# Down product of the small expert tiles: two 128-wide products in place of three, with an addition where the result leaves PSUM

## The chip, the cores and the metric

The kernel runs on one core of a Trainium2 chip as one launch. The metric is device time in microseconds (us) from the start to the end of that launch. A core has a matrix engine (PE, with its weight loads shown apart as PEld), a vector engine (DVE), a scalar engine (ACT), a general engine (POOL), and SP, which here only issues transfers. Each engine works through its own instruction stream in order, and they meet at semaphores. Matrix products end in PSUM, which has eight banks of 128 partitions by 512 fp32 values; everything else lives in SBUF.

## The reference

The program is two blocks after one another, on 256 tokens of width 1024 (and, in the second block, 256 context tokens). The first block is two layers of a swiglu network, retention and forgetting attention. The second is two layers of attention with a routed network behind each. The change touches only the routed network:

```
def moe_ffn(h, w_router, router_bias, w_gate, w_up, w_down):
    s = sigmoid(h @ w_router)                    # 16 experts in 4 groups; the best group, then 2 of its 4
    ...
    for e in range(N_EXPERTS):
        y = (silu(h @ w_gate[e]) * (h @ w_up[e])) @ w_down[e]      # 1024 -> 512 -> 1024
        out = out + gates[:, e:e + 1] * y
```

Layer 0 routes 512 tokens (latent and context), layer 1 routes 256. All inputs and weights are fp32.

## The kernel before

**Two-part numbers.** Every weight tile arrives as fp32 (`raw`, 128x1024, 512 KB), and is split into a rounded part `whi` (ACT, line 188) and the rest `wlo` (DVE, line 190: `wlo = raw - whi`). Activations are split the same way (`split`, lines 366 and 367). A product is then three matmuls into one bank (`mm3`, lines 334 to 336): high by high, high by low weight, low by high weight. In a matmul the activation is the stationary operand (up to 128 columns, one per token slot), and the weights stream past it as the moving operand, 512 columns at a time.

**Routed layers.** Each expert has a fixed number of slots by its rank in load: rank 0 is the fullest. Layer 0 has ten tiles of 80 to 128 slots and six of 64 (ranks 9 to 14). Layer 1 has two experts of two 128-slot tiles each (ranks 0 and 1), two of one 128-slot tile (2 and 3), four of 64 slots (4 to 7) and eight of 32 (8 to 15). Tiles of at most 64 slots are called small here; their entry in `TILES` has `None` as its fourth member. There are 6 in layer 0 and 12 in layer 1. For gate and up the small tiles already put the high and the low part of the token slots side by side as one stationary operand (line 1725, two matmuls of 2n columns); the two halves are summed later by a small matmul against a folding matrix (`folded`, line 1738).

**A step.** `moe` goes through the experts in the order of `ORDER`: layer 0 by ranks 15, 9, 0, 10, 11, 1, 12, 2, 3, 4, 5, 14, 7, 6, 13, 8; layer 1 by 4, 5, 0, 6, 7, 8, 1, 9, 10, 11, 2, 12, 3, 13, 14, 15. The step of an expert is: its gate product (four weight tiles), its up product (four), then the down product `Dn` of the expert before it (four), then the folding or transposing of its own hidden values (`trans`) and their split into `hth` and `htl` (`stored`). Where an expert has two tiles, `Dn` of the one before comes between gate and up. Where the next expert begins a new group of slots, four gathers (line 1707, a product with a one-hot matrix) are placed in the step: two before `Dn` and two behind it.

**Order of work.** `between` converts at most one more weight tile ahead (`pump`) each time PE is given a weight tile, so in each engine's stream the conversions stand between everything else: twelve `whi` on ACT and twelve `wlo` on DVE for every expert. At most five converted tiles are ahead of PE (`ahead`).

**The down product.** `Dn` (lines 1749 to 1778) takes two PSUM banks of the tag `acc` for each tile, which has four banks in all and is shared with the gathers. For each of four weight tiles and two halves of 512 columns it does one `mm3`: 24 matmuls. ACT then copies both halves to an SBUF tile `y` (line 1772; line 1777 in a layer's last expert), and the store of `y` to a scratch tensor `Y` is issued from ACT's own queue (line 1773). At the end of the layer, `combine` gathers each token's two rows of `Y` and adds them.

Of the kernel before, what the change touches and what calls it, by code (L numbers as in the profile page):

```python
# [25 lines left out]
FR = mybir.dt.float32r  # L26
# [3 lines left out]
OP = mybir.AluOpType  # L30
# [58 lines left out]
PLACE, TILES, RUNS = zip(*map(layout, PAIRS))  # L89
# [154 lines left out]
class Kernel:  # L244
# [1437 lines left out]
    def moe(self, l, h2):  # L1682
        nc, W, I, T = self.nc, self.W, self.I, self.T
        V, S, PE = nc.vector, nc.scalar, nc.tensor
# [47 lines left out]
        hT, T1, T2 = {}, {}, {}  # L1732

        def folded(x, n):

            q = self.bank("tr", [128, 4, n], name="fold")
            for i in range(4):
                PE.matmul(q[:, i, :], x[:2 * n, i * 128:(i + 1) * 128], self.fold[n][:2 * n], start=True, stop=True)
            return q
# [8 lines left out]
            return y  # L1748

        def stored(e, i, p, n):  # L1750
            hT[e, i] = (self.k2([128, 4, n], FR, name="hth"), self.k2([128, 4, n], FR, name="htl"))
            self.split(hT[e, i][0], hT[e, i][1], p)

        def Dn(e):
            p, ts = place[e][0], TILES[l][e]
            w = W.next(4)
            b = [[self.bank("acc", [128, 512]) for _ in range(2)] for _ in ts]
            for k in range(4):
                self.between()
                for i, t in enumerate(ts):  # L1760
                    x = hT[e, i]
                    for n in range(2):
                        c = slice(n * 512, n * 512 + 512)
                        self.mm3(b[i][n][:t[1]], (x[0][:, k, :], x[1][:, k, :]), (w[k][0][:, 0, c], w[k][1][:, 0, c]),
                                 k == 0, k == 3)
                W.rel()
            for i, (c, n, _, _) in enumerate(ts):
                rows = Y[p * 256 + c:p * 256 + c + n, :]
                if e != seq[-1]:
                    y = self.k4([128, D], name="y")  # L1770
                    for x in range(2):
                        S.copy(y[:n, x * 512:(x + 1) * 512], b[i][x][:n])
                    S.dma_start(rows, y[:n])
                else:
                    for x in range(2):
                        y = self.k2([128, 512], name="y")
                        S.copy(y[:n], b[i][x][:n])
                        S.dma_start(rows[:, x * 512:(x + 1) * 512], y[:n])
                del hT[e, i]

# [7 lines left out]
        for j, e in enumerate(seq):  # L1788
            p, ts = place[e][0], TILES[l][e]
# [14 lines left out]
            if len(ts) > 1 and last is not None:  # L1804
                self.drain()
                Dn(last)
                last = None
# [5 lines left out]
            for i, (t, q) in enumerate(zip(ts, ps)):  # L1813
                if t[3] is None:
                    hs.append(copied(q, t[1]))
                    q = folded(us[i], t[1])
# [6 lines left out]
            def trans(i, e=e, ts=ts, us=us, hs=hs):  # L1823
                n = ts[i][1]
                if ts[i][3] is None:
                    q = folded(hs[i], n)
                    V.scalar_tensor_tensor(us[i], q, 0.5, us[i], op0=OP.mult, op1=OP.mult)
                    stored(e, i, us[i], n)
                else:
                    stored(e, i, self.transp([hs[i][:n, k * 128:(k + 1) * 128] for k in range(4)]), n)  # L1830
# [4 lines left out]
            if last is not None:  # L1835
                Dn(last)
# [9 lines left out]
        W.depth(*DEPTHS["end"])  # L1846
        self.drain()
        Dn(last)
        XT.clear()
        if MORE[l] and not self.dbg.get("noov"):  # L1850
# [420 lines left out]
```

## Time and profile before

| what | us |
| --- | --- |
| three runs | 2446.01, 2446.01, 2438.97 (median 2446.01) |
| profiled execution, its own time | 2443.65 |
| its span, from first to last instruction | 2441.9 |
| PE busy, weight loads busy | 2235.7, 1792.4 |
| DVE busy | 1831.4 |
| ACT busy | 1288.0 |

The profile shows one execution. Busy time is a sum over instructions; idle time in front of an instruction is put down to the engine whose semaphore came last. Matmuls are pipelined: one of 512 columns is shown as some 390 ns long although the next may start some 230 ns after it, so the pace of PE is read from starts, not from durations. Routed layer 0 takes the stretch from about 1505 to 1810 us, routed layer 1 that from about 2095 to 2407 us.

### The profile page before, as it was taken

The numbers are of one execution on the slowest core, as the hardware profiler recorded it, in microseconds if no ns is written. First come the engines' busy times: TensorE is split into PE (matmuls) and PEld (weight loads), VectorE is DVE, ScalarE is ACT, GpSimd is POOL, SyncE is SP. The second block draws the span as 40 slices with busy tenths as digits, with TensorE's granted clock in tenths as the row PEclk, the third lists the DMA queues.
The fourth block names the chain that finished last, engine by engine and source line by source line (L and its number), as shares of the span: only waits on it lengthen the run. The fifth ranks groups of instructions, "written<-read, shape, count | busy, mean of one in ns | idle before, by whom it ended". The sixth has DMA issues, their size and how long they took to land. (4 is left out here: it accounts for less than half of the span.)

```text
span 2441.9 us, 32688 instructions
## 1 busy us (share of the span) xinstructions
PE 2235.7 (92%) x11071; PEld 1792.4 (73%) x11071; DVE 1831.4 (75%) x2734; ACT 1288.0 (53%) x1931; POOL 226.0 (9%) x533
## 2 busy tenths in 40 slices
PE   6999999999999999999998988999958977799993
PEld 5888787788788888888776767678737856677662
DVE  5787778887877766886668767888866476877796
ACT  4445454444444545444347525787855343677783
POOL 2003002000200301210100011000020011100000
PEclk9999999999999999999999998999979988899997
DMA  9786557779787657787611125999982320888994
GB/s 278 240 236 202 150 172 237 226 235 286 263 262 229 197 151 217 215 241 236 196 52 35 52 78 178 346 346 316 352 313 70 124 67 1 318 322 288 338 391 162
DMA packets 247555, 526.06 MB, mean 215 GB/s; under 512 B 22817, under 2 KB 42193, under 8 KB 247377
## 3 DMA queue, kind: packets, MB, share of 16 engines
q1 hardware_dynamic: 232160, 479.87, 61.2%
q0 software_dynamic: 9616, 29.46, 3.5%
q10 hardware_dynamic: 5601, 14.54, 1.6%
q8 instruction: 91, 1.49, 0.2%
q14 instruction: 87, 0.71, 0.1%
HBM read 503.23 MB, written 20.53 MB: 214 GB/s over the span
## 5 line engine op out<-in xcount | busy, mean ns | idle before, releaser
L190 DVE TENSOR_TENSOR wlo<-raw,whi 128x1024 fp32r<-128x1024 f32 (+1 forms) x828 | 975.5, 1209 | 184.5 <-ACT whi L188 177.0
L188 ACT CAST whi<-raw 128x1024 fp32r<-128x1024 f32 (+1 forms) x828 | 827.9, 1043 | 165.6 <-PE mm L335 39.7
L334 PE MATMUL mm<-whi,xth 128*128 128x512 f32 (+3 forms) x1152 | 445.7, 387 | 10.7 <-ACT whi L188 6.1
L336 PE MATMUL mm<-whi,xtl 128*128 128x512 f32 (+3 forms) x1152 | 431.7, 375 | 0.1
L335 PE MATMUL mm<-wlo,xth 128*128 128x512 f32 (+3 forms) x1152 | 430.6, 374 | 0.5 <-DVE wlo L190 0.5
L334 PEld LDWEIGHTS mm<-whi,xth 128*128 128x128 f32 x1152 | 218.1, 189 | 48.4 <-ACT whi L188 6.5
L334 PE MATMUL acc<-whi,hth 128*128 128x512 f32 (+4 forms) x624 | 248.0, 397 | 5.3 <-ACT whi L188 2.7
L335 PE MATMUL acc<-wlo,hth 128*128 128x512 f32 (+4 forms) x624 | 245.3, 393 | 0.5 <-DVE wlo L190 0.5
L336 PE MATMUL acc<-whi,htl 128*128 128x512 f32 (+4 forms) x624 | 245.4, 393 | 0.0
L336 PEld LDWEIGHTS mm<-whi,xtl 128*128 128x128 f32 x1152 | 217.8, 189 | 37.4 <-DVE xtl L367 2.2
L335 PEld LDWEIGHTS mm<-wlo,xth 128*128 128x128 f32 x1152 | 218.3, 190 | 32.4 <-DVE wlo L190 1.2
L957 DVE SCALAR_TENSOR_TENSOR adaacc<-adaraw,adac,adaacc 128x512 f32<-128x512 f32 x310 | 220.4, 744 | 5.7 <-DMA adaraw<-in_w_ada_dram 4.1
L334 PEld LDWEIGHTS acc<-whi,hth 128*128 128x128 f32 (+4 forms) x624 | 107.9, 173 | 39.2 <-ACT whi L188 3.0
L336 PEld LDWEIGHTS acc<-whi,htl 128*128 128x128 f32 (+4 forms) x624 | 107.7, 173 | 36.3 <-DVE htl L367 0.5
L335 PEld LDWEIGHTS acc<-wlo,hth 128*128 128x128 f32 (+4 forms) x624 | 107.8, 173 | 34.7 <-DVE wlo L190 1.5
L1725 PE MATMUL mm<-wlo,xt 128*128 128x512 f32 (+1 forms) x288 | 117.8, 409 | 13.4 <-DVE wlo L190 13.4
L366 ACT CAST hth<-tr 128x512 fp32r<-128x512 f32 (+3 forms) x64 | 35.4, 553 | 156.7 <-PE tr L362 153.2
L1725 PE MATMUL mm<-whi,xt 128*128 128x512 f32 (+1 forms) x288 | 115.7, 402 | 0.6 <-ACT whi L188 0.6
L334 PE MATMUL mm<-whi,hth 128*128 128x512 f32 x256 | 105.3, 411 | 5.0 <-DVE x L496 2.8
L305 POOL TENSOR_TENSOR rsw<-rsy 128x1 f32<-128x1 f32 (+1 forms) x75 | 26.1, 349 | 872.6 <-DVE rsy L303 856.1
L336 PE MATMUL mm<-whi,htl 128*128 128x512 f32 x256 | 102.0, 398 | 2.8 <-DVE htl L367 2.8
L335 PE MATMUL mm<-wlo,xt 128*128 128x512 f32 (+4 forms) x256 | 100.8, 394 | 2.5 <-DVE wlo L190 2.3
(460 smaller groups left out, 3410.6 us busy)
## 6 DMA issues: line engine op xcount, KB each, us to landing
raw<-in_w_ffn_in_dram SPq DMA_DIRECT2D x176, 512.0 KB, 5.5
raw<-in_w_gate_dram SPq DMA_DIRECT2D x128, 512.0 KB, 6.3
raw<-in_w_up_dram SPq DMA_DIRECT2D x128, 512.0 KB, 6.3
raw<-in_w_down_dram SPq DMA_DIRECT2D x128, 512.0 KB, 6.9
adaraw<-in_w_ada_dram SPq DMA_DIRECT2D x384, 128.0 KB, 4.9
raw<-in_w_ffn_out_dram SPq DMA_DIRECT2D x88, 512.0 KB, 6.2
raw<-in_w_in_dram SPq DMA_DIRECT2D x56, 512.0 KB, 4.6
raw<-in_wqkv_b_dram SPq DMA_DIRECT2D x20, 512.0 KB, 4.1
```

The source lines that it names most:

```text
L188: k.nc.scalar.copy(hi, lo)
L190: k.nc.vector.tensor_tensor(low, lo, hi.bitcast(FT), op=OP.subtract)
L305: newton = [lambda: g.tensor_tensor(w, y, y, op=OP.mult), lambda: g.tensor_tensor(w, w, a, op=OP.mult), lambda: g.tensor_scalar(w, w, -0.5 ...
L334: mm(out, xh, wh, start=first, stop=False)
L335: mm(out, xh, wl, start=False, stop=False)
L336: mm(out, xl, wh, start=False, stop=last)
L366: self.nc.scalar.copy(hi, src)
L957: V.scalar_tensor_tensor(a, r[:, i, :], sc, a, op0=OP.mult, op1=OP.add)
L1725: PE.matmul(o[:2 * n], x[:, i, c:c + 2 * n], a[:, i, :], start=first and q == 0, stop=last and q == 1)
```

## The change

For small tiles, `stored` puts both parts of the hidden values into one tile `hts` of 2n columns (high part first). `Dn` uses it as one stationary operand: one matmul with `whi` and one with `wlo` instead of three, so 16 matmuls for an expert instead of 24. The bank then holds two partial results, that of the high part on partitions 0 to n-1 and that of the low part on n to 2n-1. `evicted` has ACT copy the lower half to an SBUF tile `low`, and DVE add it to the upper half while reading that from PSUM. Tiles of more than 64 slots are left as they were.

```
         def stored(e, i, p, n):
-            hT[e, i] = (self.k2([128, 4, n], FR, name="hth"), self.k2([128, 4, n], FR, name="htl"))
+            if TILES[l][e][i][3] is None:
+                both = self.k2([128, 4, 2 * n], FR, name="hts")
+                hT[e, i] = (both[:, :, :n], both[:, :, n:], both)
+            else:
+                hT[e, i] = (self.k2([128, 4, n], FR, name="hth"), self.k2([128, 4, n], FR, name="htl"))
             self.split(hT[e, i][0], hT[e, i][1], p)
+        def evicted(y, p, n, stacked):
+            if stacked:
+                low = self.k2([128, 512], name="low")
+                S.copy(low[:n], p[n:2 * n])
+                V.tensor_tensor(y[:n], p[:n], low[:n], op=OP.add)
+            else:
+                S.copy(y[:n], p[:n])
...
-                        self.mm3(b[i][n][:t[1]], (x[0][:, k, :], x[1][:, k, :]), (w[k][0][:, 0, c], w[k][1][:, 0, c]),
-                                 k == 0, k == 3)
+                        if t[3] is None:
+                            for q in range(2):
+                                PE.matmul(b[i][n][:2 * t[1]], x[2][:, k, :], w[k][q][:, 0, c], start=k == q == 0,
+                                          stop=k == 3 and q == 1)
+                        else:
+                            self.mm3(b[i][n][:t[1]], (x[0][:, k, :], x[1][:, k, :]),
+                                     (w[k][0][:, 0, c], w[k][1][:, 0, c]), k == 0, k == 3)
...
-                        S.copy(y[:n, x * 512:(x + 1) * 512], b[i][x][:n])
+                        evicted(y[:, x * 512:(x + 1) * 512], b[i][x], n, d is None)
                     S.dma_start(rows, y[:n])
```

Over the program this is 144 matmuls fewer (18 experts by 8) and 36 DVE additions more (18 by 2); the number of ACT copies stays.

The first place is DVE's stream in the last steps of layer 1, from the conversions of rank 14's step to those of rank 15's. Before:

```order
L190 TENSOR_TENSOR wlo<-raw,whi 128x1024 x8
L1743 SCALAR_TENSOR_TENSOR uT<-uT,fold 128x128
L190 TENSOR_TENSOR wlo<-raw,whi 128x1024 x4
L1827 SCALAR_TENSOR_TENSOR uT<-fold,uT 128x128
L367 TENSOR_TENSOR htl<-uT,hth 128x128
```

And now:

```order
L190 TENSOR_TENSOR wlo<-raw,whi 128x1024 x8
L1743 SCALAR_TENSOR_TENSOR uT<-uT,fold 128x128
L190 TENSOR_TENSOR wlo<-raw,whi 128x1024 x4
L1764 TENSOR_TENSOR y<-acc,low 32x512 x2
L1846 SCALAR_TENSOR_TENSOR uT<-fold,uT 128x128
L367 TENSOR_TENSOR hts<-uT,hts 128x4x32
```

The two additions (L1764) stand behind the four conversions that `Dn` asked for and ahead of the two operations that finish the next expert's hidden values.

The second place is ACT's stream at the same point, with the semaphores that each row waits for in brackets. Before:

```order
L1772 COPY y<-acc 32x512 [waits DVE_49,PE_49]
L1772 COPY y<-acc 32x512 [waits PE_49]
L1773 DMA Y_84<-y 32x1024 [waits DMAHW5_49,Activation_49]
L366 CAST hth<-uT 128x128 [waits DVE_49]
L188 CAST whi<-raw 128x1024 [waits DMAHW3_49]
```

And now:

```order
L188 CAST whi<-raw 128x1024 [waits DMAHW2_49,DVE_49,PE_49]
L1763 COPY low<-acc 32x512 [waits PE_49] x2
L1792 DMA Y_84<-y 32x1024 [waits DMAHW5_49,DVE_49]
L366 CAST hts<-uT 128x4x32 [waits DVE_49]
L188 CAST whi<-raw 128x1024 [waits DMAHW3_49,Activation_49]
```

The store's issue waited for ACT's own copies, and now waits for DVE's additions, with the cast of the hidden values and the next conversions behind it.

The third place is PE's stream behind `Dn` of a small tile in a step with gathers (rank 7 in layer 1): the two gathers behind `Dn`, each of two banks (`h2h`, then `h2l`). Before:

```order
L1707 MATMUL xg<-oh,h2h 128x256 [waits Activation_49]
L1707 MATMUL xg<-oh,h2h 128x256 x3
L1707 MATMUL xg<-oh,h2l 128x256 [waits Activation_49]
L1707 MATMUL xg<-oh,h2l 128x256 x3
L1707 MATMUL xg<-oh,h2h 128x256 [waits Activation_49]
L1707 MATMUL xg<-oh,h2h 128x256 x3
L1707 MATMUL xg<-oh,h2l 128x256 [waits Activation_49]
L1707 MATMUL xg<-oh,h2l 128x256 x3
```

And now:

```order
L1707 MATMUL xg<-oh,h2h 128x256 [waits Activation_49]
L1707 MATMUL xg<-oh,h2h 128x256 x3
L1707 MATMUL xg<-oh,h2l 128x256 [waits Activation_49]
L1707 MATMUL xg<-oh,h2l 128x256 x3
L1707 MATMUL xg<-oh,h2h 128x256 [waits DVE_49]
L1707 MATMUL xg<-oh,h2h 128x256 x3
L1707 MATMUL xg<-oh,h2l 128x256 [waits DVE_49]
L1707 MATMUL xg<-oh,h2l 128x256 x3
```

The last gather takes over the two banks that `Dn` has just filled. It waited for ACT to copy them out, and now waits for DVE's additions.

## Rows read from the trace of the kernel before

**Rows 1.** The page's first part: busy us, share of the span, instructions.
```profile
PE 2235.7 (92%) x11071; PEld 1792.4 (73%) x11071; DVE 1831.4 (75%) x2734; ACT 1288.0 (53%) x1931; POOL 226.0 (9%) x533
```
**Rows 2.** Windows: stretch, length, busy us and count by engine, PE clock, DMA share, GB/s.
```profile
1505.00:1810.00 305.00, 290.22 (x1403) 220.64 (x1402) 257.18 (x283) 236.44 (x308) 10.38 (x14) 0.97 0.93 332
2095.00:2407.00 312.00, 302.78 (x1447) 211.89 (x1445) 251.40 (x276) 242.92 (x319) 1.69 (x3) 0.99 0.91 333
```
**Rows 3.** Timeline, PE, rank 6 of layer 1: start, us, what, idle before.
```profile
2189.56 0.44 PE L334 MATMUL acc<-whi,hth 128*64 128x512 f32 x1
...
2195.13 0.63 PE L1707 MATMUL xg<-oh,h2h 128*128 128x256 f32 x4
...
2196.07 0.64 PE L1707 MATMUL xg<-oh,h2h 128*128 128x256 f32 x4
```
**Rows 4.** Timeline, PE, ranks 3 and 13 of layer 1: two matmuls 22 apart; folds.
```profile
2361.72 0.40 PE L335 MATMUL acc<-wlo,hth 128*128 128x512 f32 x1
...
2366.73 0.39 PE L336 MATMUL acc<-whi,htl 128*128 128x512 f32 x1
2367.05 1.07 PE L1738 MATMUL fold<-fold,gs 64*128 64x32 f32 x8
...
2382.45 1.07 PE L1738 MATMUL fold<-fold,gs 64*128 64x32 f32 x8
```
**Rows 5.** Timeline, DVE, the step of rank 14 in layer 1.
```profile
2370.28 9.21 DVE L190 TENSOR_TENSOR wlo<-raw,whi 128x1024 fp32r<-128x1024 f32 x8 [0.66 <-ACT whi L188]
2379.40 0.28 DVE L1743 SCALAR_TENSOR_TENSOR uT<-uT,fold 128x128 f32<-128x128 f32 x1
2379.60 4.62 DVE L190 TENSOR_TENSOR wlo<-raw,whi 128x1024 fp32r<-128x1024 f32 x4
2384.14 0.28 DVE L1827 SCALAR_TENSOR_TENSOR uT<-fold,uT 128x128 f32<-128x128 f32 x1
2385.11 0.29 DVE L367 TENSOR_TENSOR htl<-uT,hth 128x128 fp32r<-128x128 f32 x1 [0.69 <-ACT hth L366]
2386.06 9.17 DVE L190 TENSOR_TENSOR wlo<-raw,whi 128x1024 fp32r<-128x1024 f32 x8 [0.66 <-ACT whi L188]
```
**Rows 6.** Windows of eight steps with a small down product and no gathers; their sum.
```profile
1527.10:1544.90 17.80, 16.45 (x73) 11.31 (x72) 17.80 (x17) 14.37 (x17) 0.00 (x0) 1.00 1.04 398
...
2370.30:2386.10 15.80, 15.80 (x76) 8.72 (x75) 14.45 (x16) 13.86 (x19) 0.00 (x0) 1.00 1.04 397
...
sum 131.70, PE 127.76 PEld 80.84 DVE 121.96 ACT 109.74 POOL 1.06; mean PE 15.97 PEld 10.10 DVE 15.24 ACT 13.72 POOL 0.13
```
**Rows 7.** Window of a step of a two-tile expert behind a small one.
```profile
2132.80:2159.00 26.20, 26.20 (x122) 20.36 (x120) 17.55 (x17) 14.32 (x17) 0.00 (x0) 1.00 0.79 266
```
**Rows 8.** Timeline, DVE and ACT, the same small down product as Rows 3.
```profile
2190.60 4.85 DVE L190 TENSOR_TENSOR wlo<-raw,whi 128x1024 fp32r<-128x1024 f32 x4
2194.64 1.27 ACT L1772 COPY y<-acc 64x512 f32<-64x512 f32 x2 [0.83 <-PE acc L336]
...
2196.45 1.05 ACT L188 CAST whi<-raw 128x1024 fp32r<-128x1024 f32 x1 [0.55 <-ACT y L1772]
```
**Rows 9.** Timeline, DVE and PE, rank 4 of layer 1.
```profile
2123.45 4.62 DVE L190 TENSOR_TENSOR wlo<-raw,whi 128x1024 fp32r<-128x1024 f32 x4
...
2127.17 0.64 PE L1707 MATMUL xg<-oh,h2h 128*128 128x256 f32 x4
```
**Rows 10.** A DVE addition from PSUM and SBUF elsewhere: ns minimum, median, maximum.
```profile
L1435 DVE TENSOR_TENSOR y<-mm,row x10: 678/691/692, 1392.4 to 2056.6; 128x512 f32<-128x512 f32 x10
```
**Rows 11.** Timeline, PE, the step of rank 11 in layer 1.
```profile
2289.59 0.44 PE L1725 MATMUL mm<-wlo,xt 128*64 128x512 f32 x1 [0.99 <-DVE wlo L190]
```
**Rows 12.** Window and PE timeline in layer 0, behind waits for `wlo`.
```profile
1552.00:1556.00 4.00, 4.00 (x15) 3.54 (x14) 4.00 (x4) 0.76 (x2) 0.00 (x0) 0.50 1.05 387
1557.40 0.63 PE L335 MATMUL acc<-wlo,hth 128*128 128x512 f32 x1
1557.83 0.63 PE L336 MATMUL acc<-whi,htl 128*128 128x512 f32 x1
```

More of the change, by code (lines that the diff above doesn't have):

```diff
@@ L1763, in Dn @@
                         c = slice(n * 512, n * 512 + 512)
-                        self.mm3(b[i][n][:t[1]], (x[0][:, k, :], x[1][:, k, :]), (w[k][0][:, 0, c], w[k][1][:, 0, c]),
-                                 k == 0, k == 3)
+                        if t[3] is None:
[5 more added lines that the diff above has]
+                                     (w[k][0][:, 0, c], w[k][1][:, 0, c]), k == 0, k == 3)
                 W.rel()
-            for i, (c, n, _, _) in enumerate(ts):
+            for i, (c, n, _, d) in enumerate(ts):
                 rows = Y[p * 256 + c:p * 256 + c + n, :]
@@ L1776, in Dn @@
                         y = self.k2([128, 512], name="y")
-                        S.copy(y[:n], b[i][x][:n])
+                        evicted(y, b[i][x], n, d is None)
                         S.dma_start(rows[:, x * 512:(x + 1) * 512], y[:n])
```

## The prediction

> **What bounds the kernel now.** I read the page's busy times first. PE is busy 92% of the span, DVE 75%, ACT 53% [rows 1], which speaks for a change that takes matmuls away. But that is a mean over stages, and matmul durations overlap, so I went on to the windows of the two routed layers, the only stages touched. In layer 0 PE is busy 290.22 of 305 us and DVE 257.18; in layer 1 it is 302.78 of 312 and 251.40 [rows 2]. The reader is to see two things: PE has hardly a gap there, yet DVE follows at 81 to 84%, and the transfers run at 332 GB/s. So I cut the layers into the steps of single experts, by the timeline. They are of different kinds. In eight steps with a small down product and no gathers, DVE is busy 121.96 of 131.70 us, and in the fullest of them all of the time; transfers are at 397 to 398 GB/s there [rows 6]. In the step of a two-tile expert DVE is busy only 17.55 of 26.20 us and transfers drop to 266 GB/s [rows 7]. The bound changes from step to step, and the saving has to be booked step by step.
>
> The end of layer 1 shows how close the engines are. From the fold behind one down product to the fold behind the next PE takes 2382.45 - 2367.05 = 15.40 us [rows 4]. DVE's own round takes 2386.06 - 2370.28 = 15.78 us, and in it conversions stand without a gap except for a short chain: finish the hidden values, wait for ACT's cast, subtract, wait for the next `whi` (0.69 and 0.66 us) [rows 5]. That chain is a dependency and not slack. The transfers need 12 x 0.524 MB at 397 GB/s [rows 6], 15.85 us, for the same round. Three resources tie, and a lighter PE alone moves none of the other two.
>
> **The change part by part.**
>
> *Matmuls removed.* 24 products of 64 or fewer stationary columns take 2195.13 - 2189.56 = 5.57 us, 0.232 each [rows 3]. Products with 128 columns start (2366.73 - 2361.72) / 22 = 0.228 us apart [rows 4], so 16 of them are 3.64 us. I take 1.9 us off PE per small expert, 18 x 1.9 = 34 us in all. This is what the change is worth if PE is the last to be ready everywhere.
>
> *Additions added.* The nearest row is DVE's addition from PSUM and SBUF at line 1435, 0.691 us for 128x512 [rows 10], and I take the same for 32 and 64 partitions, since an instruction's columns follow one another and its partitions don't. Successive DVE instructions overlap a little (eight `wlo` take 9.21 us), so two additions hold DVE for 1.25 us, between 1.2 and 1.4. Over 18 experts that is 22 us of DVE. Behind an addition on DVE are queued the two operations that finish the next expert's hidden values, and then the conversions that PE needs next. The ACT copies stay as many and as long; I cost them at nothing. The store's issue on ACT's queue now waits for DVE, with the cast and conversions behind it, priced in the classes below. The strided cast and subtraction into `hts` have the same number of elements and are costed at nothing (bounds -0.1 and +0.1 us each). One k2 buffer more is used per small expert; the ring has 21, and I cost this at nothing.
>
> *Class a, two small down products inside the step of a two-tile expert (ranks 5 and 8 in layer 1).* DVE idles a third of this step [rows 7] and hides the additions; PE runs through. Each gives back 1.9 us: -3.8.
>
> *Class b, seven in steps with gathers (layer 0: 10, 12, 14; layer 1: 4, 6, 7, 10).* The last gather needs the banks that `Dn` filled. Rank 6: `Dn` would end at 2193.2 instead of 2195.13; the gather ahead takes 0.94 us. But DVE's four conversions last until 2190.60 + 4.85 = 2195.45 [rows 8], the additions can only follow, and free the banks at about 2196.05 and 2196.65. Before, that gather started at 2196.07 [rows 3]. PE runs to the wait 1.9 us earlier and stands there for it: 0 gained. Rank 4 is worse: conversions until 2123.45 + 4.62 = 2128.07, first bank free at 2128.7 where the gather started at 2127.17 [rows 9], so +1.5. In layer 0 a gather has twice the matmuls (four token tiles), so the wait is covered longer, and rank 10, where DVE is ahead, can gain up to 1.45. Value taken: 0 for the class. Bounds: 7 x -1.45 = -10 and 7 x 1.5 = +10.5.
>
> *Class c, eight in steps where DVE is full (layer 0: 9, 11, 13; layer 1: 9, 11, 12, 13, 14).* Here the additions lengthen DVE's round by 1.25 us, and PE, which catches up with the conversions a few matmuls later as it does today (0.99 us of waiting for `wlo` at 2289.59 [rows 11]), ends up that much later: the 1.9 us it saved become waiting. DVE is idle 131.70 - 121.96 = 9.74 us in the eight [rows 6], 1.2 each, of which the dependency chain of 0.66 and 0.69 us [rows 5] takes nearly all. I take +1.1 for each, +8.8. Bounds: 0, if all that idle time can absorb them, and +2 each (+16), if ACT's wait for the additions delays the next `whi` as well.
>
> *Class d, the last small expert (rank 15).* Nothing but the chain to the end is left: 1.9 us less of matmuls, 0.3 more before them, since the first one now needs the low part too (0.29 us [rows 5]), and one addition of 0.7 behind the last copy: -0.9.
>
> Sum: -3.8 + 0 + 8.8 - 0.9 = +4.1 us on the profiled execution's own 2443.65, so 2447.8, about 2448. That execution lies 2.4 us under the median of the runs shown, 2446.01, and inside their spread, so against the median the forecast is +0.1%, no change that can be told: this kernel's measurement tells about 0.3%, 7.3 us, here from 2438.7 to 2453.3. By the bounds: -3.8 - 10 + 0 - 0.9 = -14.7 (2429) and 0 + 10.5 + 16 + 0 = +26.5 (2470).
>
> **The rivals.**
>
> *PE stays the bound.* For it: PE is busy 593 of 617 us in the two layers [rows 2], and up to five converted tiles stand ahead of it, so a late DVE need not be felt at once; each two-tile or gather step refills that lead. Then the additions fit into idle time, and classes a, b and d give 10 x 1.9 = 19 us while c gives 0: 2425. Against it: the waits in rows 8 and 11 show a lead that is used up already. The full 34 us (2410) would need c to gain as well, against transfers at 397 GB/s [rows 6].
>
> *The store's issue holds up ACT.* ACT now stands at the issue until DVE has added. In class b its next `whi` started at 2196.45 [rows 8]; the additions alone last until 2196.65, so with the issue behind them it starts some 0.7 us later, and where DVE is further behind, as at rank 4 (additions until 2129.3, 2.1 us behind the start of the gather that they free [rows 9]), some 2 us later. If each such delay comes back as a late conversion, the 15 steps of b and c cost 2 us each instead of 0 and 1.1: 30 - 3.8 - 0.9, 2469. It decides from the point at which the five tiles' lead is gone, which in class c is soon and in b often covered by the gathers.
>
> *The clock falls.* In layer 0, behind repeated waits for `wlo`, the granted clock went to 0.50 and products started 0.43 us apart (1557.83 - 1557.40) instead of 0.228 [rows 12]: the lower level, 1.2 GHz against 2.4. With the change PE waits 3 us of 16.7 in every class c step, in short pieces. If the clock falls in four of the eight, with some 15 products at 0.43 each time, 4 x 15 x 0.2 = 12 us come on top of the forecast: 2460. Against it: in the fullest class c step PE already waits 1.35 of 17.80 us at a clock of 1.00 [rows 6], and a slower product costs nothing where PE would have waited for `wlo` anyway. The Trainium skill, TensorE: Matmul & The Clock Gate, section "Loop structure matters more than you think", has the same rule: products broken up by waits run cold. By that rule the trace agrees at 0.50, and the time would be this rival's.
>
> That the change does not do what it says is out: the instruction order shows 16 products per small expert and the additions in place.
>
> **How the numbers follow.** Forecast (DVE eats PE's gain) 0.58; PE stays the bound 0.20; ACT held 0.12; clock 0.10. Faster by over 0.3% (under 2438.7): nearly all of the second case, 0.18, and 0.04 of the forecast's spread, 0.22. Slower by over 0.3% (over 2453.3): the two slow cases, 0.20, and 0.06 of the forecast, 0.26. Within: 0.52. The forecast's own range is 2437 to 2457 (b and c off by 10 us together). The range that leaves a tenth out on either side reaches to the middle of the fast case and the clock's case: 2429 to 2462.
>
> **What would show it.** Right: routed layers as long as before within some 5 us; DVE over 95% busy in the class c steps with PE waiting for `wlo`; in class b the last gather waiting for L1764; the two-tile steps 1.9 us shorter; ACT's issue of the store waiting for DVE. Wrong: PE still without gaps in class c and the layers shorter by 15 us or more; additions well over 0.7 us; `whi` late by 2 us behind every store; or a PE clock under 0.9 in class c windows.

## The result: 0.65% slower

Seven runs of the changed kernel have a median of 2459.66 us (2453.68 to 2464.84), seven of the kernel before 2444.99 (2438.97 to 2446.01). The ratio is 1.0065, 95% interval 1.0050 to 1.0081: slower by 15.9 us, between 12.2 and 19.8. The profiled execution took 2458.36 us (span 2456.2, clock 0.958) against 2443.65 (span 2441.9, clock 0.963). The time lies inside the predicted range (to 2462), but not where the likeliest case had put it (2448).

The page of the changed kernel answers [rows 1]: PE has 144 matmuls and 15 us less, DVE 36 instructions and 21 us more, ACT is unchanged.

```profile
PE 2220.9 (90%) x10927; PEld 1793.5 (73%) x10927; DVE 1852.3 (75%) x2770; ACT 1287.3 (52%) x1931; POOL 223.9 (9%) x533
```

Up to 1460 us the two traces agree (PE's busy time there differs by 3 us in 1390). Windows of the two routed layers, up to the end of the last down product, first before, then after (columns as in [rows 2]):

```profile
1505.00:1809.00 304.00, 290.22 (x1403) 220.64 (x1402) 257.18 (x283) 235.86 (x307) 10.38 (x14) 0.97 0.93 333
2097.70:2406.30 308.60, 300.08 (x1435) 209.67 (x1433) 248.91 (x267) 239.79 (x314) 1.69 (x3) 0.99 0.91 334
```

```profile
1505.00:1815.70 310.70, 285.95 (x1347) 221.10 (x1346) 263.90 (x295) 235.55 (x307) 8.51 (x14) 0.96 0.92 326
2100.60:2418.70 318.10, 288.90 (x1343) 209.48 (x1342) 262.37 (x294) 240.11 (x315) 1.69 (x3) 0.97 0.89 325
```

Add up length minus PE: PE was idle 22.3 us before and 53.95 after, 31.7 more, while its busy time fell by only 15.5 (590.3 to 574.85), although 144 matmuls at 0.228 are 33 us. A part of that difference is clock: the granted mean went from 0.97 and 0.99 to 0.96 and 0.97, and slower matmuls count as busy; by these rounded means it is some 10 us, an estimate. 31.7 - 15.5 is the 16.2 us by which the layers got longer. So the saving is there; PE spends all of it, and as much again, in waiting.

What PE waits for in layer 1 is named by the list of waits (us in all, times, longest). Before, it held 6.6 us for `wlo`, 1.2 for `hth` and 0.6 for `whi`; after:

```profile
PE mm L1725 <- DVE wlo L190: 10.5, 14, 1.1
PE xg L1707 <- DVE y L1764: 8.4, 4, 3.6
PE mm L1725 <- ACT whi L188: 5.1, 4, 1.3
```

And the view of the additions' own line (L1764; duration in ns, then who waited for it) shows that ACT waits for them longest:

```profile
L1764 DVE TENSOR_TENSOR y<-acc,low x36: 668/673/680, 1544.7 to 2420.5; 64x512 f32<-64x512 f32 x20, 32x512 f32<-32x512 f32 x16
...
  ACT whi L188: 19.7, 8
  ACT hth L366: 12.4, 4
  PE xg L1707: 10.7, 7
```

Four places show how.

*Class c, rank 9 of layer 0.* Timeline of ACT, DVE and PE (start, us, what, idle before and releaser):

```profile
1540.64 1.07 ACT L1763 COPY low<-acc 64x512 f32<-64x512 f32 x2
1545.96 0.50 ACTq L1792 DMA_DIRECT2D Y<-y  x1
1546.51 0.58 ACT L366 CAST hth<-tr 128x512 fp32r<-128x512 f32 x1 [4.80 <-DVE y L1764]
...
1540.12 4.63 DVE L190 TENSOR_TENSOR wlo<-raw,whi 128x1024 fp32r<-128x1024 f32 x4
1544.65 1.28 DVE L1764 TENSOR_TENSOR y<-acc,low 64x512 f32<-64x512 f32 x2
1547.12 0.69 DVE L367 TENSOR_TENSOR htl<-tr,hth 128x512 fp32r<-128x512 f32 x1 [1.19 <-ACT hth L366]
...
1548.09 0.49 PE L1725 MATMUL mm<-whi,xt 128*128 128x512 f32 x1 [2.33 <-ACT whi L188]
```

ACT copies at 1540.64 and has nothing to do until 1545.96: the additions stand on DVE behind four conversions (4.63 us), and ACT stands at the store's issue. The cast behind it is late, then DVE's subtraction (1.19 us idle on the engine that bounds the step), then `whi`, then PE. In the kernel before, DVE went from its conversions straight into that subtraction, with no idle time:

```profile
1539.76 4.62 DVE L190 TENSOR_TENSOR wlo<-raw,whi 128x1024 fp32r<-128x1024 f32 x4
1544.30 0.68 DVE L367 TENSOR_TENSOR htl<-tr,hth 128x512 fp32r<-128x512 f32 x1
```

*Class b, rank 4 of layer 1* (answers [rows 9]). PE and DVE:

```profile
2128.38 0.63 PE L1707 MATMUL xg<-oh,h2l 128*128 128x256 f32 x4
2132.57 0.74 PE L1707 MATMUL xg<-oh,h2h 128*128 128x256 f32 x4 [3.56 <-DVE y L1764]
...
2127.30 4.63 DVE L190 TENSOR_TENSOR wlo<-raw,whi 128x1024 fp32r<-128x1024 f32 x4
2131.84 1.28 DVE L1764 TENSOR_TENSOR y<-acc,low 64x512 f32<-64x512 f32 x2
```

The bank's release hangs on the same four conversions: 3.56 us of waiting, and the clock is down behind it (0.76 over the window 2133 to 2140).

*Rank 6 of layer 1* (answers [rows 3]). The down product lasts 2198.84 - 2195.06 = 3.78 us instead of 5.57, the 1.8 us of the forecast, and the next gather stands for 1.64 of them:

```profile
2195.06 0.50 PE L1780 MATMUL acc<-whi,hts 128*128 128x512 f32 x1
...
2198.84 0.64 PE L1707 MATMUL xg<-oh,h2h 128*128 128x256 f32 x4
...
2201.59 0.74 PE L1707 MATMUL xg<-oh,h2h 128*128 128x256 f32 x4 [1.64 <-DVE y L1764]
```

*Class d, the end of layer 1.* Ranks 14 and 15, PE, ACT and DVE:

```profile
2407.03 1.07 PE L1738 MATMUL fold<-fold,gs 64*128 64x32 f32 x8
2412.84 0.69 PE L1780 MATMUL acc<-whi,hts 128*64 128x512 f32 x1 [4.73 <-DVE hts L367]
...
2412.16 0.30 ACT L366 CAST hts<-uT 128x128 fp32r<-128x128 f32 x1 [2.75 <-DVE uT L1846]
...
2405.97 4.62 DVE L190 TENSOR_TENSOR wlo<-raw,whi 128x1024 fp32r<-128x1024 f32 x4
2410.51 1.27 DVE L1764 TENSOR_TENSOR y<-acc,low 32x512 f32<-32x512 f32 x2
2411.71 0.27 DVE L1846 SCALAR_TENSOR_TENSOR uT<-fold,uT 128x128 f32<-128x128 f32 x1
```

From the fold to the last down product it now takes 5.81 us; before it took 2.31, with 1.25 of waiting. After 4.73 idle microseconds the first ten matmuls start 0.43 us apart, at the lower clock.

The last row to answer is DVE's own round in the step of rank 14 of layer 1 [rows 5]. It takes 2396.68 - 2379.91 = 16.77 us, before 15.78: +0.99, against the +1.1 of the forecast. The sign "DVE over 95% busy" is not met: the window of this round (last line, columns as in [rows 2]) has DVE busy 15.60 of 16.77 us, 93%.

```profile
2379.91 9.18 DVE L190 TENSOR_TENSOR wlo<-raw,whi 128x1024 fp32r<-128x1024 f32 x8 [0.66 <-DMA raw<-in_w_gate_dram]
...
2393.75 1.27 DVE L1764 TENSOR_TENSOR y<-acc,low 32x512 f32<-32x512 f32 x2
...
2396.68 2.36 DVE L190 TENSOR_TENSOR wlo<-raw,whi 128x1024 fp32r<-128x1024 f32 x2 [0.65 <-ACT whi L188]
...
2379.91:2396.68 16.77, 15.52 (x74) 9.24 (x72) 15.60 (x18) 13.97 (x19) 0.00 (x0) 1.00 1.04 399
```

To sum by the prediction's classes, I took the start of every down product in both traces, and for each small expert the growth of the shift up to the next one's start. These are sums over single executions:

```
class a  (L1 5, 8)                       -1.8 -1.8                                  = -3.6
class b  (L0 10 12 14; L1 4 6 7 10)      -1.4 -0.6 -0.5 +4.4 +0.9 +0.1 +0.1         = +3.0
class c  (L0 9 11 13; L1 9 11 12 13 14)  +1.9 +2.2 +4.2 +1.4 +2.0 +1.9 +0.7 +1.7    = +15.9
class d  (L1 15, to the end)                                                        = +2.0
steps without the change, and routing                                               = -3.0
sum (2456.2 - 2441.9)                                                               = +14.3
```

### The profile page after: what moved, and what is told of

Read it like the earlier page. It is cut to its first block, busy times and chain, and to the rows that moved or that the text cites. A ratio compares the mean times of both kernels' runs of the same rounds, so it can differ in the third digit from the quotient of the medians.

```text
span 2456.2 us, 32445 instructions
## 1 busy us (share of the span) xinstructions
PE 2220.9 (90%) x10927; PEld 1793.5 (73%) x10927; DVE 1852.3 (75%) x2770; ACT 1287.3 (52%) x1931; POOL 223.9 (9%) x533
## 5 line engine op out<-in xcount | busy, mean ns | idle before, releaser
L334 PE MATMUL acc<-whi,hth 128*128 128x512 f32 (+4 forms) x480 | 190.5, 397 | 7.2 <-ACT hth L366 6.0
L335 PE MATMUL acc<-wlo,hth 128*128 128x512 f32 (+4 forms) x480 | 188.1, 392 | 0.8 <-DVE wlo L190 0.8
L336 PE MATMUL acc<-whi,htl 128*128 128x512 f32 (+4 forms) x480 | 188.2, 392 | 0.0
L1725 PE MATMUL mm<-wlo,xt 128*128 128x512 f32 (+1 forms) x288 | 123.1, 427 | 17.3 <-DVE wlo L190 17.2
L1725 PE MATMUL mm<-whi,xt 128*128 128x512 f32 (+1 forms) x288 | 120.7, 419 | 9.5 <-ACT whi L188 9.5
L334 PEld LDWEIGHTS acc<-whi,hth 128*128 128x128 f32 (+4 forms) x480 | 89.6, 187 | 27.1 <-ACT hth L366 6.2
L335 PEld LDWEIGHTS acc<-wlo,hth 128*128 128x128 f32 (+4 forms) x480 | 89.7, 187 | 20.4 <-DVE wlo L190 1.1
L336 PEld LDWEIGHTS acc<-whi,htl 128*128 128x128 f32 (+4 forms) x480 | 89.5, 186 | 20.4 <-issue 0.5
```

The source lines that it names most:

```text
L334: mm(out, xh, wh, start=first, stop=False)
L335: mm(out, xh, wl, start=False, stop=False)
L336: mm(out, xl, wh, start=False, stop=last)
L1725: PE.matmul(o[:2 * n], x[:, i, c:c + 2 * n], a[:, i, :], start=first and q == 0, stop=last and q == 1)
```

## The experiments

Theory A: the additions on DVE cost, by their time and their place behind the conversions. Theory B: the store's issue on ACT costs, because ACT waits there for the additions. Differences in us are the ratio's, at 2444 us, with the 95% interval.

**e1: the matmuls by themselves.**

```
-                low = self.k2([128, 512], name="low")
-                S.copy(low[:n], p[n:2 * n])
-                V.tensor_tensor(y[:n], p[:n], low[:n], op=OP.add)
+                S.copy(y[:n], p[:n])
```

> Stacked products as in the changed kernel, but neither the copy of the lower rows nor the addition: only the upper rows of the bank are copied (the low part of the hidden units times the weights is left out), and the store waits for ACT alone as before. It prices the matmuls by themselves. Theory A (the additions sit in DVE's queue behind weight splits, and whoever waits for them is late: they alone turn the gain round) and theory B (the store's issue waits for the additions on ACT's queue, and the casts of ACT behind it are late) both expect faster than before, 2420 to 2437 us. Rival C (the layers are held by the weight splits anyway, so that fewer matmuls bring nothing): 2442 to 2448. Rival D (the stacked products themselves run slower, by clock or weight loads): 2455 or more.

Measured: 2431.07, ratio 0.9941 (0.9924 to 0.9958), -14.4 us (-18.6 to -10.3). C and D fall. But of 33 us of matmuls only 14 come out, with no addition anywhere. Summed by class as above, e1's trace has -3.7 in a, -12.0 in b and +3.0 in c: in class c fewer matmuls bring nothing in sum, even by themselves. At the end of each layer PE is only earlier at hidden values that aren't ready. It waited 1.34 and 1.25 us for them in the kernel before, in e1 it waits (end of layer 0, then of layer 1):

```profile
1796.62 0.71 PE L334 MATMUL acc<-whi,hth 128*80 128x512 f32 x1 [4.57 <-ACT hth L366]
2388.41 0.69 PE L1778 MATMUL acc<-whi,hts 128*64 128x512 f32 x1 [3.39 <-DVE hts L367]
```

In the changed kernel these two waits are 6.04 and 4.73 us. What stands ahead of the hidden values are conversions: in layer 0 each `whi` just ahead waits 0.22 to 0.26 us for its own transfer, in layer 1 four `wlo` take 4.62 us.

**e2: the additions by themselves.**

```
-                        if t[3] is None:
-                            for q in range(2):
-                                PE.matmul(b[i][n][:2 * t[1]], x[2][:, k, :], w[k][q][:, 0, c], ...
+                        self.mm3(b[i][n][:t[1]], (x[0][:, k, :], x[1][:, k, :]), ...
...
-                S.copy(low[:n], p[n:2 * n])
+                S.copy(low[:n], p[:n])
```

> The three products of the kernel before, with the copy and the addition of the changed kernel put on top (the copy takes the same rows, so these output rows come out doubled). A and B: the additions' whole cost without the gain, 2465 to 2485 us. C: about the changed kernel's time, 2458 to 2462, since the matmuls brought nothing. D: faster than the changed kernel, 2445 to 2452.

Measured: 2462.9, ratio 1.0083 (1.0069 to 1.0096), +20.3 us (16.9 to 23.5); as a time 2 us below the range of A and B, and near what C expected, but e1 rules C out. The two halves add to +5.9, the change measures +15.9: 10 us, some 3.5 to 16.5 with the intervals added in squares, come only when both are there. The steps say where. By class, from the starts of the down products in the three traces (single executions):

```
              a      b      c      d   other    sum
e1         -3.7  -12.0   +3.0    0.0   +0.5  -12.2
e2          0.0   +5.5  +15.5   +1.2   -4.1  +18.1
change     -3.6   +3.0  +15.9   +2.0   -3.0  +14.3
```

In class b, e1 and e2 add to -6.5 and the change has +3.0; a, d and the others add to within 1 us, and c comes out 2.6 lower than its sum. The last gather of class b starts when both PE and the bank are ready. With fewer matmuls alone PE comes earlier and finds the bank free; with additions alone the bank is late, but in most steps PE is too; with both, PE waits. It waits 10.7 us in 7 places for the additions at the gathers of the changed kernel (the line of L1764 above), and e1 has no additions to wait for. The same view of e2:

```profile
  PE xg L1707: 2.3, 1
```

The clock fell as well: its mean over the runs is 0.963 before, 0.9615 in e1, 0.961 in e2 and 0.957 in the changed kernel. A part of the 10 us may be its; these runs don't part it from the waits.

**e3: the same stores from POOL's queue.**

```
-                    S.dma_start(rows, y[:n])
+                    (nc.gpsimd if d is None else S).dma_start(rows, y[:n])
```

> The changed kernel, with the stores of the small tiles issued by POOL instead of ACT; POOL is nearly idle in the layers. Everything else stays, the additions on DVE too. B: ACT no longer waits (19.7 us ahead of whi in 8 places and 12.4 us ahead of hth in 4 in the changed kernel), and most of the loss goes: 2430 to 2448 us. A: nothing changes but the place of the issue, 2455 to 2462.

Measured: 2450.64, ratio 1.0038 (1.0025 to 1.0052), +9.3 us. Between the two theories: the move takes 6.6 of the 15.9 us away (some 1.5 to 11.5 with the intervals added in squares), and more than half of the loss stays.

**e4: the addition on POOL as well.**

```
+                low, high = self.k2([128, 512], name="low"), self.k2([128, 512], name="high")
+                S.copy(high[:n], p[:n])
                 S.copy(low[:n], p[n:2 * n])
-                V.tensor_tensor(y[:n], p[:n], low[:n], op=OP.add)
+                nc.gpsimd.tensor_tensor(y[:n], high[:n], low[:n], op=OP.add)
```

> As the run before it (store issued by POOL), and the addition itself moved to POOL: ACT copies both halves out of PSUM (36 copies more, 0.58 us each, 21 us of ACT's time in all), POOL adds them in SBUF. DVE then has no work of the change and the banks wait for ACT alone. A: the loss goes here and not in the run before: 2425 to 2440. B: no better than the run before it, within 3 us. If ACT becomes the bound by its 21 us: 2455 or more.

Measured: 2447.25, ratio 1.0017 (1.0007 to 1.0027), +4.2 us. By the ratios 5 us better than e3, so not B's "within 3", but far from A's 2425 to 2440, and the time is under the 2455 that was set for ACT's 36 further copies. Neither theory alone gives this, and e4 is no clean test of A. In its trace POOL's addition takes 1.72 us (median of 36) where DVE's took 0.673; DVE, with as many instructions as before (2734), is busy 1843.2 us instead of 1831.4; and POOL comes late to the gathers at the end of layer 0 (see the last section). What ACT's copies cost besides, no run here shows.

**e5 and e6: the change for one half of the experts each.** `STACK` lists the ranks by layer; e5 has ((10, 12, 14), (4, 5, 6, 7, 8, 10)), e6 ((9, 11, 13), (9, 11, 12, 13, 14, 15)).

```
-            if TILES[l][e][i][3] is None:
+            if e in STACK[l] and TILES[l][e][i][3] is None:
```

> The change for 9 of the 18 small experts alone: ranks 10, 12, 14 of layer 0 and 4, 5, 6, 7, 8, 10 of layer 1 (those inside a two-tile step or a step with gathers); the other nine keep three products and plain copies. The prediction's terms: -3.8 for ranks 5 and 8, 0 for the gather steps, so 2439 to 2443. The profile of the changed kernel, step by step (shift of one down product's start to the next one's): -3.6 and +3.0, so 2441 to 2446. If the loss is spread over all steps alike (half of 15 us): 2449 to 2453.

> The other nine alone: ranks 9, 11, 13 of layer 0 and 9, 11, 12, 13, 14, 15 of layer 1. The prediction's terms: +8.8 - 0.9, so 2450 to 2453. The profile of the changed kernel step by step: +15.9 + 1.9, so 2457 to 2463. If the loss is spread alike: 2449 to 2453 as well. With the run before it, the two differences to the kernel before should add up to the change's 15 to 16 us; if they add up to much less, the rest is a clock that falls when both are there.

Measured: e5 2447.22, ratio 1.0020 (1.0010 to 1.0029), +4.9 us; e6 2460.79, ratio 1.0073 (1.0060 to 1.0085), +17.8 us. The loss isn't spread alike: classes c and d alone are as slow as the whole change. The halves add to 22.7, more than the 15.9 of both, not less. e5 lies in none of its three ranges.

**e7: a candidate, a part of a and b with POOL's issue.** `STACK` is ((10, 12, 14), (5, 6, 7, 8)), the issue as in e3.

> The candidate: the change for ranks 10, 12, 14 of layer 0 and 5, 6, 7, 8 of layer 1, with their stores issued by POOL. By the steps of the run with POOL's issue (-1.4, -0.5, -0.5 and -1.9, -0.6, +0.1, -1.9): -6.7, so 2434 to 2440. If the clock falls with any stall that the additions leave: 2441 to 2447.

Measured: 2441.9, ratio 0.9991 (0.9981 to 1.0000), -2.2 us. Not the 7 us that the steps promised; they had been read from e3's profiled execution, the fastest of its six (2444.97, median 2450.64). The time lies in the range set for a falling clock; the mean clock is 0.9615.

**e8: classes c and d with POOL's issue.** `STACK` as in e6, the issue as in e3.

> The change for the nine small experts of classes c and d alone, as two runs before, with their stores issued by POOL. Theory B (in these steps it is ACT, held at the store's issue until DVE has come to the additions, that costs): most of the excess over the prediction's +7.9 goes, 2448 to 2453. Theory A (DVE's own additions and their place in its queue): 2457 to 2462, as with ACT's issue.

Measured: 2451.85, ratio 1.0034 (1.0021 to 1.0047), +8.3 us. It lies in B's range; 9.5 of e6's 17.8 us go. The end of layer 0 shows the place. Timeline of ACT and DVE there in the changed kernel, with the issue on ACT:

```profile
1803.96 1.07 ACT L1763 COPY low<-acc 64x512 f32<-64x512 f32 x2
1806.42 0.45 ACTq L1792 DMA_DIRECT2D Y<-y  x1
1806.92 0.42 ACT L366 CAST hth<-tr 128x320 fp32r<-128x320 f32 x1 [1.88 <-DVE y L1764]
...
1807.37 0.49 DVE L367 TENSOR_TENSOR htl<-tr,hth 128x320 fp32r<-128x320 f32 x1 [0.98 <-ACT hth L366]
```

And in e8 (its lines are numbered one higher), where the cast follows the copies at once and DVE goes from the additions into the subtraction without a gap:

```profile
1800.62 1.07 ACT L1764 COPY low<-acc 64x512 f32<-64x512 f32 x2
1801.71 0.43 ACT L367 CAST hth<-tr 128x320 fp32r<-128x320 f32 x1
...
1802.80 1.27 DVE L1765 TENSOR_TENSOR y<-acc,low 64x512 f32<-64x512 f32 x2
1804.00 0.47 DVE L368 TENSOR_TENSOR htl<-tr,hth 128x320 fp32r<-128x320 f32 x1
```

**e9 and e10: controls, the kernel before with POOL's issue.** e9 moves the stores of the small tiles (`d is None`), e10 all of them.

```
-                    S.dma_start(rows, y[:n])
+                    (nc.gpsimd if d is None else S).dma_start(rows, y[:n])
```

> A control: the kernel before, with nothing changed but that the stores of the same 18 small tiles are issued by POOL. If what POOL's issue gave the changed kernel is the wait for the additions (B), there is no such wait here and the time stays: 2440 to 2445. If any store's issue on ACT costs (its own 0.3 us and its wait for the copy), it gets faster by as much as the changed kernel did, 2434 to 2438.

> The kernel before with all stores of the routed experts issued by POOL. By B no change (2440 to 2445); if ACT's issues cost by themselves, 2430 to 2438.

Measured: e9 2439.5, ratio 0.9979 (0.9970 to 0.9987), -5.1 us; e10 2447.91, ratio 1.0012 (1.0003 to 1.0021), +2.9. Neither lies in a range given for it. e9 goes against B as I had put it: the move brings 5.1 us where ACT waits for no addition. Against e9, the change with POOL's issue (e3) costs 1.0038 / 0.9979, +14.4 us, about as much as against the kernel before with ACT's.

**e11: e7 with all stores from POOL.** The store's line reads `nc.gpsimd.dma_start(rows, y[:n])` for every expert.

> The candidate of the run with nine experts' (a and b) change and POOL's issue, with the stores of all other experts issued by POOL too. By B as that candidate, 2440 to 2444; if ACT's issues cost by themselves, 2430 to 2437.

Measured: 2446.12, ratio 1.0003 (0.9994 to 1.0011), no difference to be told, above both ranges, and 3 us above e7; e10 is 8 us above e9.

**e12: the control to e8.** The kernel before, POOL's issue for `STACK` of e6 alone.

> The control to the run with the change for classes c and d and POOL's issue: the kernel before, where the stores of the same nine experts alone are issued by POOL. There the move brought 9.7 us (2460.8 to 2451.9, against +18.0 and +8.3 to the kernel before). Theory B (what the move brings is that ACT need not wait for the additions): without additions it brings at most half of what it brought for all eighteen (5.1), so 2441 to 2444. If the move brings the same without additions, because any store's issue on ACT costs that much: 2433 to 2437, and B falls.

Measured: 2439.65, ratio 0.9983 (0.9975 to 0.9992), -4.2 us. Neither theory's number. Of the 9.5 us that the move brings in classes c and d, 4.2 come without additions, and 5.3 (about 0.5 to 10 with the intervals added in squares) are the wait for the additions. The steps of class c agree: the move takes them from +13.2 (e6) to +2.8 (e8), and without additions (e12) from 0 to -1.9. Over all eighteen experts, though, the same comparison (e3, e9) leaves 6.6 - 5.1 = 1.5 us for that wait, within the noise. The other part of the loss doesn't care where the store is issued: e8 against e12 is 1.0034 / 0.9983, +12.5 us. In the two traces 4.7 of it lie in class c's steps and 7.2 between the last down product of layer 0 and the first of layer 1; what causes those isn't settled.

## Why the prediction was wrong in its likeliest case

*Matmuls removed:* right. 16 matmuls in 3.78 us; 14 of the 18 down products are shorter by 1.8 to 1.9 us, ranks 9 and 13 of layer 0 and 4 of layer 1 by less, and that of rank 15, at the lower clock, is as long as before (5.44 us from first to last start, before 5.31). But what became of the time differs by class: e1 shows it given back in a and b, and nothing of it in c.

*Additions:* right in size. 0.673 us each where 0.691 was taken, 1.27 for two. What the forecast left to the classes is where they stand.

*Class a:* right. -3.6 in the trace for -3.8.

*Class b:* 0 forecast, +3.0 in the trace, inside the bounds. The mechanism was right, the last gather waits for L1764. Rank 4 is the odd one, +4.4 for +1.5. Its wait had been sized rightly: the bank free at 2128.7 and PE there at 2127.17 - 1.9, 3.4 us, measured 3.56. Left out was the clock behind such a stall: that gather and the fold take 2135.29 - 2132.57 = 2.72 us where they took 1.78, and the next four matmuls start 0.42 to 0.57 us apart. Timed alone (e5), a and b make +4.9, 8.7 above the terms' -3.8. e5's own trace has -3.6 and +2.1 for them, which accounts for 2 of that; +4.8 stand in the steps of ranks 11 and 13 of layer 0, which e5 leaves as they were, and why isn't settled.

*Class c is the step that failed:* +8.8 forecast, +15.9 in the trace, and with class d +17.8 timed (e6) for +7.9. "I take +1.1 for each" holds for DVE's round where nothing else is late (+0.99 at rank 14) but left out ACT. The upper bound had named it: "+2 each (+16), if ACT's wait for the additions delays the next `whi` as well". It does: ACT idles 4.80 us at rank 9 of layer 0, and the cast of `hth`, which DVE itself needs next, sits behind the issue as well. e8 and e12 show that this is part of it (5.3 of 17.8) and that it is not all.

*Class d:* -0.9 forecast, +2.0 in the trace. "Nothing but the chain to the end is left" was wrong. Four conversions and rank 14's additions are still ahead of rank 15's hidden values on DVE, and PE, idle for 4.73 us, starts the last product at the lower clock. The conversions are the greater part: without any addition (e1) the wait is 3.39 us.

*The rivals.* PE stays the bound (2425): out; e1 shows that even without additions less than half of the matmuls' time comes back. ACT held (2469): its mechanism is there, 32 us of ACT waiting for L1764 before `whi` and `hth`, but a part of these waits costs nothing. The clock (2460): its time is nearest, and the clock did fall in more places. The shortfall from full clock, (1 - clock) x span, is 90 us in the mean of the runs before and 106 after. Within the seven runs of the changed kernel, too, the one at 0.960 took 2453.68 and the one at 0.953 2464.84. Windows show it low behind waits that came with the change: 0.76 behind rank 4 of layer 1 (above), 0.51 from 1806 to 1813, behind the 6.04 us at the end of layer 0, and 0.61 from 2410 to 2418.7, behind the 4.73 us; in the kernel before, the same places have 1.00. At rank 9 of layer 0 it is 0.59 from 1552 to 1558, but it was 0.50 there before [rows 12]. The Trainium skill (TensorE: Matmul & The Clock Gate, "Loop structure matters more than you think") has matmuls that stand apart by long waits run cold; these rows agree. But the fall follows waits that A and B cause, and no run here kept the clock up while leaving the waits, so its own share stays open.

*The range* held, with luck. 2459.66 lies outside the forecast's own range (to 2457); the stated one reaches to 2462 only for the clock's case, which is not shown to be the cause.

What settled: the additions cost 20 us (e2) where the matmuls bring 14 (e1). The costly place is classes c and d (e6); in c the matmuls bring nothing even alone (e1), and ACT's wait at the issue is one part of the cost (e8, e12). The 10 us between e1 plus e2 and the whole stand in class b by the traces, at the gathers. Open are the rest of class c's cost beside ACT's wait, and the clock's own share.

## What to carry to other kernels

When a result's last step moves to another engine, price the wait by what that engine has queued ahead at that moment in the new order (here four conversions, 4.6 us), not by the step's own 0.67 us; then list what stands behind the instruction that waits. Saved matmul time counts only in steps where the other engines have room: 33 us removed gave 14 with nothing added. Where a saving on one engine and a cost on another meet at one wait, as at class b's gathers, two runs that time them apart don't add up to both. And before keeping such a change, try its side edit alone: the fastest kernel here that leaves nothing out, e9 at 0.9979 (0.9970 to 0.9987; e12 can't be told from it), has none of the change.

## What the runs showed that I had not expected

Issuing the small tiles' stores from POOL makes the kernel before faster by 5.1 us, although ACT waits there for no other engine at the issue; issuing all of them there gives the gain back and 2.9 us more. A reason for the second stands at the end of layer 0. There the combine's gather (L1863) is issued by POOL behind the last store. Before, with the store on ACT, 4.3 us lie between the store's issue (1809.93 + 0.32) and the first gather:

```profile
1809.93 0.32 ACTq L1778 DMA_DIRECT2D Y<-y  x1
...
1814.57 1.07 POOL L1863 DMA_INDIRECT yr<-Y,rtri  x1 [29.11 <-SPq L1923]
```

In e10 both are on POOL, and 13.5 us lie between them:

```profile
1800.95 1.24 POOL L1778 DMA_DIRECT2D Y<-y  x2 [7.07 <-ACT y L1777]
...
1815.64 1.07 POOL L1863 DMA_INDIRECT yr<-Y,rtri  x1 [1.03 <-issue]
```

In e9, where this last store stays on ACT, it is 5.8 us:

```profile
1802.44 0.32 ACTq L1778 DMA_DIRECT2D Y<-y  x1
...
1808.59 1.09 POOL L1863 DMA_INDIRECT yr<-Y,rtri  x1 [1.00 <-issue]
```

So e10's last down product is early and its gather isn't. POOL's own stream shows why: between the store and the gather stand loads of small tensors (L1062) and small operations on them (L1981 to L1983) that wait for them. In e10:

```profile
1802.90 0.93 POOL L1062 DMA_DIRECT2D lgc<-in_ln_ffn_g_dram  x1 [0.71 <-issue]
...
1809.85 0.20 POOL L1981 TENSOR_TENSOR ca<-sc,lgc 128x8 f32<-128x8 f32 x1 [3.39 <-DMA sc<-mod]
...
1813.67 0.20 POOL L1981 TENSOR_TENSOR ca<-sc,lgc 128x8 f32<-128x8 f32 x1 [1.36 <-DMA sc<-mod]
```

In the kernel before, POOL had no stores to stand at and was through with this work early:

```profile
1783.92 1.10 POOL L1981 TENSOR_TENSOR ca<-sc,lgc 128x8 f32<-128x8 f32 x1 [4.97 <-DMA sc<-mod]
```

In e9 it stands behind the store of rank 13 (1794.94), and so is done by 1807.58. The runs with the change and POOL's issue pay for this too: from the last store's issue to the first gather e3 takes 6.2 us, e4 10.2 and e8 5.6, the changed kernel 3.0. Where e9's 5 us come from, no run here shows.
